# Transposing the widening layers' outputs on VectorE instead of TensorE

## The chip, the cores and the metric

The kernel runs on one core of a Trainium2 chip, in one launch. The metric is the device time of one execution in microseconds (us). The matrix products run on TensorE (PE; its weight loads are listed apart as PEld), the elementwise work on VectorE (DVE) and ScalarE (ACT), a few small things on GpSimd (POOL), and the weights come in over DMA queues that SyncE (SP) starts.

## The reference

Two transformer blocks are computed one after the other on 256 tokens of width 2048, all in float32. What matters for this change are the two feed-forward parts, one at the end of each block; everything else (gated linear attention, forgetting attention, sparse attention, pooling, memory attention) is left as it is.

```
h = h + (o * gate) @ w_out
u = jax.nn.relu(rms_norm(h, mlp_norm_g) @ w_up)          # 2048 -> 8192
h = h + (u * u) @ w_down                                  # 8192 -> 2048
...
h = rms_norm_2(x, ln_ffn_pre[l])
y = (jax.nn.silu(h @ w_gate[l]) * (h @ w_up[l])) @ w_down[l]   # 2048 -> 5632 -> 2048
x = x + rms_norm_2(y, ln_ffn_post[l])
```

## The kernel before

**The products.** Every weight matrix is read once from HBM, in units of 1024 columns per partition (two blocks of 128 rows by 512 columns, 512 KB). A unit lands in one of five raw buffers (`raw`), ScalarE rounds it into `wh` (line 133, type float32r), VectorE computes the rest `wl = raw - wh` (line 366), and the pair goes into one of six pairs of buffers. The activations are split into a high part H and a low part L in the same way. TensorE then does three products for each block and each half of the tokens: H by wh (line 460), H by wl (461) and L by wh (462), each 128x512. A unit is therefore 2 blocks x 2 halves x 3 = 12 matmuls. The pair is free for a later unit when its last matmul (462) is done.

**The feed-forward parts.** The first one (`up`, `down`) has 16 groups `up0` to `up15` of 512 output columns, each with 16 blocks (8 units), and after every second pair of them a set of four groups `dn` with 16 units, in which the outputs of an earlier pair are multiplied by `w_down`. So the outputs of `up` groups 2b and 2b+1 are used after the groups 2b+2 and 2b+3 have been multiplied. The second part (`ffn_gate`, `ffn_up`, `ffn_down`, names `fg`, `fu`, `fd`) has 11 groups of gate and up columns and is arranged in the same way.

**What is transposed.** A widening group leaves its result with the tokens on the partitions, and the narrowing product needs it with the columns on the partitions. So each of the 27 outputs (16 + 11), 256 tokens by 512 columns, goes through `T_split`: in two halves, four transposes each of a 128x128 block on TensorE into a PSUM bank `pb` (line 203), then a copy to the high part by ScalarE (`split_T`, `self.act(hi, ps)`) and a subtraction for the low part by VectorE (`self.tt(lo, ps, hi)`), both 128x512 out of PSUM. Before it, `up` applies Relu on ScalarE (two 128x512) and squares on VectorE (128x1024); `ffn_up` multiplies on VectorE.

**The order.** The program is written out by a Python planner. The matmuls of the products follow a fixed list of units. Between two blocks `pump` advances tasks (Python generators; a `yield` ends a step), guarded by rough costs (`dv`, `act`, `tr`) that the planner adds up for each engine: it takes steps of a task while the planned times of ScalarE and VectorE are less than 3500 ns ahead of the planned time of TensorE. `more` splits the next units, up to four ahead of the one in use. Each engine then runs its own instructions strictly in that order, and waits at semaphores for the others. Scratch tiles `s` of 128x1024 come from an arena of 32.

Of the kernel before, what the change touches and what calls it, by code (L numbers as in the profile page):

```python
# [10 lines left out]
F32 = mybir.dt.float32  # L11
F32R = mybir.dt.float32r
I32 = mybir.dt.int32
AF = mybir.ActivationFunctionType
OP = mybir.AluOpType
# [93 lines left out]
class Program:  # L109
# [399 lines left out]
    def T_split(self, nat, gain, hi, lo):  # L509
        h3, l3 = v3(hi, 4), v3(lo, 4)  # L510

        def sink(half, ps):
            s = slice(2 * half, 2 * half + 2)
            self.split_T(ps, None if gain is None else gain[:, s], h3[:, s], l3[:, s])

        yield from self.T_group(nat, sink)

    def T_plain(self, nat, dst, gain=None):
        d3 = v3(dst, 4)

        def sink(half, ps):
            s = slice(2 * half, 2 * half + 2)
            if gain is None:
                self.copy(d3[:, s], ps)
            else:
                self.scopy(d3[:, s], ps, gain)

        yield from self.T_group(nat, sink)
# [59 lines left out]
def v3(f, a):  # L588
    return f.rearrange("p (a b) -> p a b", a=a)


class Kernel(Program):
# [472 lines left out]
    def up(self, banks, j):  # L1065
        yield from self.until(("rs", "h"))
        rs = self.rs["h"]
        (f,) = yield from self.F.wait()
        f3 = v3(f, 2)
        for t in range(2):  # L1070
            self.act(f3[:, t], banks[t], AF.Relu, scale=rs[:, t:t + 1])
        if j == 15:
            self.free_TT("h")
        yield "B"
        self.tt(f, f, f, OP.mult)
        yield 1
        yield from self.u_T(f3, j, 2)
        self.F.put(f)

    def u_T(self, f3, j, per):  # L1080
        h, l = yield from self.R.wait(2)
        yield from self.T_split(f3, None, h, l)
        H, L = self.TT.setdefault(("u", j // per), ([None] * per, [None] * per))
        H[j % per], L[j % per] = h, l
        self.ev.add(("u", j))

    def down(self, banks, b, c):
# [546 lines left out]
    def ffn_up(self, banks, j):  # L1634
        yield from self.until(("g", j))
        f = self.S.pop(("g", j))
        f3 = v3(f, 2)
        for t in range(2):
            self.stt(f3[:, t], banks[t], self.rs["hf"][:, t:t + 1], f3[:, t], OP.mult, OP.mult)
        if j == 10:  # L1640
            self.free_TT("hf")
        yield "B"
        h, l = yield from self.R.wait(2)
        yield from self.T_split(f3, None, h, l)
        self.F.put(f)
        b, k, n = j // 2, j % 2, 2 if j < 10 else 1
        H, L = self.TT.setdefault(("w", b), ([None] * n, [None] * n))
        H[k], L[k] = h, l
        self.ev.add(("w", j))
# [109 lines left out]
    def build(self):  # L1759
# [105 lines left out]
        def inter(up, dn, nb, per):  # L1865
            seq = list(up(0))
            for b in range(nb):
                seq += list(up(b + 1)) if b + 1 < nb else []
                seq += dn(b)
            return seq  # L1870
# [276 lines left out]
```

## Time and profile before

| | |
|---|---|
| median of 3 runs | 2641.49 us (2641.45 to 2643.71) |
| the profiled execution | 2642.02 us |
| its span in the profile | 2640.3 us |
| PE busy | 2616.5 us (99%), 12196 matmuls |
| DVE busy | 1504.9 us (57%), 1921 instructions |
| ACT busy | 1251.9 us (47%), 1708 instructions |
| POOL busy | 76.5 us (3%) |
| DMA, mean | 189 GB/s |
| granted TensorE clock, mean | 0.998 |

The span runs from the first to the last instruction of the program, and the execution's own time is 1.7 us longer. A share of busy time is a mean over the whole span. A matmul's duration is its way through the pipeline, so consecutive matmuls overlap; how fast TensorE really goes is read from the distance between starts in the timeline. A row of the timeline gives the start, the time, the engine, the line, the operation, out<-in and a count, and in brackets the idle time of the engine before it and what ended that.

### The profile page before, as it was taken

To read this page: it belongs to the slowest core of one execution; us is meant where nothing else is said; L and a number is where in the kernel's file an instruction comes from. 1 tells how busy PE (TensorE), PEld (TensorE's weight loads), DVE (VectorE), ACT (ScalarE), POOL (GpSimd) and SP (SyncE) were. 2 spreads that over 40 slices of the span, in tenths; PEclk is the share of its full clock that TensorE was granted. 3 is DMA by queue.
4 is the path that set the end of the run, shared out by engine and by line. 5 is a ranking of instruction groups with operands and counts; after the bars stand their busy time and mean duration, and the time that the engine had idled before them with its cause. 6 is when DMAs were issued, how large, how long until landed. Compare 5 with 4: busy or idle time off the path is not lost.

```text
span 2640.3 us, 32053 instructions
## 1 busy us (share of the span) xinstructions
PE 2616.5 (99%) x12196; PEld 2168.9 (82%) x12196; DVE 1504.9 (57%) x1921; ACT 1251.9 (47%) x1708; POOL 76.5 (3%) x97
## 2 busy tenths in 40 slices
PE   9999999999999999999999999999999999999998
PEld 7888888888888888888888888888788888888886
DVE  6567655555555555555566545666755455555555
ACT  7544544444444444444455344465554444444443
POOL 0001000000000000001000000000100000000001
PEclk9999999999999999999999999999999999999999
DMA  9643565555566565555444557555455555556553
GB/s 343 204 139 119 166 216 185 188 188 184 191 201 223 187 223 195 191 202 198 150 143 147 190 177 258 201 199 184 136 193 189 192 188 194 186 195 202 195 186 129
DMA packets 138891, 500.18 MB, mean 189 GB/s; under 512 B 15650, under 2 KB 16594, under 8 KB 138737
## 3 DMA queue, kind: packets, MB, share of 16 engines
q1 hardware_dynamic: 131760, 473.16, 53.0%
q0 software_dynamic: 6976, 24.98, 2.7%
q8 instruction: 95, 1.56, 0.2%
q14 instruction: 60, 0.48, 0.1%
HBM read 493.33 MB, written 7.88 MB: 190 GB/s over the span
## 4 chain that ended last, share of the span: by engine, by line
PE 94%; issue 4%; DVE 1%; ACT 0%; DMA 0%; POOL 0%; SPq 0%; DVEq 0%; ACTq 0%; POOLq 0%
PE gb L460 29%; PE gb L462 29%; PE gb L461 29%; PE pb L197 4%; PE pb L203 3%; DVE wl L366 0%; DVE s L169 0%; DMA s<-memT 0%; DVE s L158 0%; POOL st L232 0%; ACT wh L133 0%; PE gb L451 0%; ACT s L133 0%; PE gb L450 0%; PE gb L452 0%
## 5 line engine op out<-in xcount | busy, mean ns | idle before, releaser
L366 DVE TENSOR_TENSOR wl<-raw,wh 128x1024 fp32r<-128x1024 f32 (+1 forms) x876 | 1052.8, 1219 | 689.5 <-ACT wh L133 687.4
L460 PE MATMUL gb<-wh,s 128*128 128x512 f32 x3496 | 1383.9, 396 | 2.2 <-ACT wh L133 2.1
L461 PE MATMUL gb<-wl,s 128*128 128x512 f32 x3496 | 1362.5, 390 | 2.5 <-DVE wl L366 2.5
L462 PE MATMUL gb<-wh,s 128*128 128x512 f32 x3496 | 1363.4, 390 | 0.0
L133 ACT ACTIVATE wh<-raw 128x1024 fp32r<-128x1024 f32 (+1 forms) x878 | 914.0, 1055 | 802.2 <-PE gb L462 766.8
L462 PEld LDWEIGHTS gb<-wh,s 128*128 128x128 f32 x3496 | 656.4, 188 | 139.3 <-DVE s L169 0.5
L460 PEld LDWEIGHTS gb<-wh,s 128*128 128x128 f32 x3496 | 657.2, 188 | 137.4 <-ACT wh L133 3.7
L461 PEld LDWEIGHTS gb<-wl,s 128*128 128x128 f32 x3496 | 657.5, 188 | 135.1 <-DVE wl L366 4.2
L158 DVE TENSOR_TENSOR s<-gb,s 128x512 f32<-128x512 f32 x144 | 98.1, 691 | 159.6 <-PE gb L462 130.5
L133 ACT ACTIVATE s<-pb 128x512 fp32r<-128x512 f32 (+4 forms) x171 | 89.4, 536 | 163.6 <-PE pb L203 139.5
L133 ACT ACTIVATE s<-gb,st 128x512 f32<-128x512 f32 (+1 forms) x112 | 70.0, 642 | 199.5 <-PE gb L462 188.0
L197 PE MATMUL pb<-s,s 128*128 128x128 f32 (+4 forms) x720 | 116.5, 301 | 1.3 <-DVE s L158 0.9
L203 PE MATMUL pb<-cc,s 128*128 128x128 f32 x700 | 106.0, 274 | 5.4 <-DVE s L169 5.3
L203 PEld LDWEIGHTS pb<-cc,s 128*128 128x128 f32 x700 | 87.0, 141 | 29.0 <-DVE s L169 6.6
L197 PEld LDWEIGHTS pb<-s,s 128*128 128x128 f32 x720 | 97.7, 191 | 9.5 <-DVE s L158 1.3
L158 DVE TENSOR_TENSOR s<-pb,s 128x512 fp32r<-128x512 f32 (+4 forms) x87 | 57.5, 664 | 62.4 <-ACT s L133 58.6
L133 ACT ACTIVATE s<-pb,vecs 128x256 fp32r<-128x256 f32 (+2 forms) x109 | 42.3, 453 | 49.9 <-PE pb L203 40.5
L163 DVE TENSOR_SCALAR s<-gb,st 128x512 f32<-128x512 f32 (+1 forms) x32 | 20.9, 658 | 67.8 <-PE gb L462 51.5
L169 DVE SCALAR_TENSOR_TENSOR s<-pb,vecs,s 128x256 fp32r<-128x256 f32 (+1 forms) x104 | 40.0, 435 | 29.0 <-ACT s L133 29.0
L133 ACT ACTIVATE s<-s,st 128x128 f32<-128x128 f32 (+2 forms) x73 | 32.8, 450 | 31.7 <-DVE st L163 30.4
L133 ACT ACTIVATE s<-s 128x512 f32<-128x512 f32 (+3 forms) x46 | 37.0, 807 | 21.5 <-DVE s L158 12.4
L232 POOL TENSOR_TENSOR st<-st,nhalf 128x8 f32<-128x8 f32 (+2 forms) x21 | 26.1, 1243 | 689.5 <-DVE st L165 689.5
(113 smaller groups left out, 565.0 us busy)
## 6 DMA issues: line engine op xcount, KB each, us to landing
raw<-w_in SPq DMA_DIRECT2D x216, 512.0 KB, 4.2
raw<-w_up SPq DMA_DIRECT2D x216, 512.0 KB, 4.4
raw<-w_down SPq DMA_DIRECT2D x216, 512.0 KB, 4.4
raw<-w_gate SPq DMA_DIRECT2D x88, 512.0 KB, 4.6
raw<-w_out SPq DMA_DIRECT2D x32, 512.0 KB, 4.5
raw<-w_mix_out SPq DMA_DIRECT2D x32, 512.0 KB, 4.6
raw<-w_br_pool SPq DMA_DIRECT2D x16, 512.0 KB, 5.2
raw<-w_br_attn SPq DMA_DIRECT2D x16, 512.0 KB, 4.1
```

Of the source, the lines that this page charges most:

```text
L133: self.nc.scalar.activation(out, in_, func, **kw)
L158: self.nc.vector.tensor_tensor(out, a, b, op)
L163: self.nc.vector.tensor_scalar(out, a, s1, None, op0=op0)
L169: self.nc.vector.scalar_tensor_tensor(out, a, s, b, op0, op1)
L197: self.nc.tensor.matmul(out, lhsT, rhs, start=start, stop=stop)
L203: self.nc.tensor.transpose(out, in_, self.ident[:k, :k])
L232: self.nc.gpsimd.tensor_tensor(r, t, self.nhalf[:, :k], op=OP.pow)
L366: self.nc.vector.tensor_sub(l[:, :m], r, h[:, :m].bitcast(F32))
L460: mm(o, H[:, c:c + 128], wh, start=st, stop=False)
L461: mm(o, H[:, c:c + 128], wl, start=False, stop=False)
L462: mm(o, L[:, c:c + 128], wh, start=False, stop=sp)
```

## The change

A new function `T_dve` takes the place of `T_split` for the 27 outputs. It takes one more scratch tile `g`, and fills it with 16 transposes on VectorE. Each reads 32 partitions (quarter `a` of the tokens of a half) and 256 elements of each (8 pieces of 32), turns each block of 32 by 32, and writes it to 32 partitions of quarter `q` of `g`. After every second of them the step ends. Then ScalarE makes the high part from `g` and VectorE the low part, now 128x1024 in one piece and out of SBUF. In `up` the square is taken on ScalarE and no longer on VectorE.

```
+    def T_dve(self, f, hi, lo):
+
+        (g,) = yield from self.F.wait()
+        x = f.rearrange("p (t k q j) -> p k t q j", t=2, k=4, q=4)
+        y = g.rearrange("p (k t a i) -> p k t a i", k=4, t=2, a=4)
+        for a in range(4):
+            for q in range(4):
+                self.nc.vector.transpose(y[32 * q:32 * q + 32, :, :, a], x[32 * a:32 * a + 32, :, :, q])
+                self.dv(256)
+                if q % 2:
+                    yield 1
+        self.F.put(f)
+        self.act(hi, g)
+        yield 1
+        self.tt(lo, g, hi.bitcast(F32), OP.subtract)
+        self.F.put(g)
...
     def up
-        self.tt(f, f, f, OP.mult)
+        self.act(f, f, AF.Square)
         yield 1
-        yield from self.u_T(f3, j, 2)
-        self.F.put(f)
...
+        yield from self.T_dve(f, h, l)
...
     def ffn_up
-        yield from self.T_split(f3, None, h, l)
-        self.F.put(f)
+        yield from self.T_dve(f, h, l)
```

On TensorE the order of the changed kernel is the order before without 54 rows of four transposes; no other row moves there. POOL's and SP's orders are the same. The place shown on TensorE is the first half of the output of `up0`, between two products of 128x512 (`gb` is a product's PSUM bank, `wh` and `wl` the weight pair, `cc` holds the identity, `s_115` is the output of `up0`):

```order
 L462 MATMUL gb_83<-wh_70,s_108_2865 128x512
-L203 MATMUL pb_87<-cc,s_115_3407 128x128 x4
 L460 MATMUL gb_82<-wh_72,s_109_3006 128x512
 L461 MATMUL gb_82<-wl_73,s_109_3006 128x512
```

The row of four transposes is gone and the products close up.

On VectorE the same place, the output `s_115` of `up0`, reads before (the square, then the two low parts `s_117` out of the banks `pb`, among the low parts `wl` of the weights):

```order
L366 TENSOR_TENSOR wl_77<-raw_69,wh_76 128x1024
L158 TENSOR_TENSOR s_115_3407<-s_115_3407 128x1024
L366 TENSOR_TENSOR wl_79<-raw_65,wh_78 128x1024
L366 TENSOR_TENSOR wl_81<-raw_66,wh_80 128x1024
L158 TENSOR_TENSOR s_117_3442<-pb_87,s_116_3441 128x512
L158 TENSOR_TENSOR s_117_3442<-pb_89,s_116_3441 128x512
L366 TENSOR_TENSOR wl_71<-raw_67,wh_70 128x1024
```

and in the changed kernel (`s_118` is the tile `g`, `s_116` the high part):

```order
L366 TENSOR_TENSOR wl_79<-raw_65,wh_78 128x1024
L525 STREAM_TRANSPOSE s_118_3437<-s_115_3407 32x8x32 x2
L366 TENSOR_TENSOR wl_81<-raw_66,wh_80 128x1024
L525 STREAM_TRANSPOSE s_118_3437<-s_115_3407 32x8x32 x4
L366 TENSOR_TENSOR wl_71<-raw_67,wh_70 128x1024
L525 STREAM_TRANSPOSE s_118_3437<-s_115_3407 32x8x32 x4
L366 TENSOR_TENSOR wl_73<-raw_68,wh_72 128x1024
L525 STREAM_TRANSPOSE s_118_3437<-s_115_3407 32x8x32 x2
L366 TENSOR_TENSOR wl_75<-raw_69,wh_74 128x1024
L525 STREAM_TRANSPOSE s_118_3437<-s_115_3407 32x8x32 x4
L366 TENSOR_TENSOR wl_77<-raw_65,wh_76 128x1024
L158 TENSOR_TENSOR s_117_3436<-s_118_3437,s_116_3435 128x1024
```

The square has left this engine, and 16 transposes in pieces of two or four now stand between the low parts of five units of weights, with the low part of the output behind the sixth.

## Rows read from the trace of the kernel before

**Rows 1.** The page's first part: busy time, share of the span and instructions of each engine.

```profile
PE 2616.5 (99%) x12196; PEld 2168.9 (82%) x12196; DVE 1504.9 (57%) x1921; ACT 1251.9 (47%) x1708; POOL 76.5 (3%) x97
```

**Rows 2.** Busy time in two stretches, most of the first feed-forward part and most of the second: the length, then busy us and number of instructions of PE, PEld, DVE, ACT and POOL, the granted clock, the DMA share and GB/s.

```profile
450.00:1110.00 660.00, 660.00 (x2980) 545.94 (x2980) 361.01 (x348) 289.80 (x316) 9.23 (x16) 1.00 0.58 196
1980.00:2580.00 600.00, 600.00 (x2687) 496.97 (x2686) 307.95 (x288) 251.81 (x259) 1.14 (x2) 1.00 0.58 192
```

**Rows 3.** The timeline of PE around the transposes of one output of `up`, from the fourth matmul ahead of the first four transposes to the fifteenth behind the second four.

```profile
1013.65 0.39 PE L461 MATMUL gb<-wl,s 128*128 128x512 f32 x1
...
1014.56 0.39 PE L462 MATMUL gb<-wh,s 128*128 128x512 f32 x1
1014.79 0.60 PE L203 MATMUL pb<-cc,s 128*128 128x128 f32 x4
1015.14 0.48 PE L460 MATMUL gb<-wh,s 128*128 128x512 f32 x1
1015.46 0.40 PE L461 MATMUL gb<-wl,s 128*128 128x512 f32 x1
...
1016.62 0.60 PE L203 MATMUL pb<-cc,s 128*128 128x128 f32 x4
...
1019.12 0.39 PE L460 MATMUL gb<-wh,s 128*128 128x512 f32 x1
```

**Rows 4.** The groups of instructions in the same stretch (1013.83 to 1019.13 us, with the matmul that started at 1013.65 still running): count, busy us and mean ns.

```profile
L460 PE MATMUL gb<-wh,s 128*128 128x512 f32 x7 | 2.9, 415 | 0.0
L462 PE MATMUL gb<-wh,s 128*128 128x512 f32 x7 | 2.8, 393 | 0.0
L461 PE MATMUL gb<-wl,s 128*128 128x512 f32 x7 | 2.7, 391 | 0.0
L203 PE MATMUL pb<-cc,s 128*128 128x128 f32 x8 | 1.2, 272 | 0.0
```

**Rows 5.** The timeline of ACT soon after, with nothing but the weights' high parts to do.

```profile
1021.36 1.06 ACT L133 ACTIVATE wh<-raw 128x1024 fp32r<-128x1024 f32 x1 [1.61 <-PE gb L462]
1024.08 1.06 ACT L133 ACTIVATE wh<-raw 128x1024 fp32r<-128x1024 f32 x1 [1.66 <-PE gb L462]
1026.80 1.06 ACT L133 ACTIVATE wh<-raw 128x1024 fp32r<-128x1024 f32 x1 [1.66 <-PE gb L462]
```

**Rows 6.** The timeline of DVE, from the square of that output to the weights behind it.

```profile
1005.20 1.23 DVE L366 TENSOR_TENSOR wl<-raw,wh 128x1024 fp32r<-128x1024 f32 x1 [1.50 <-ACT wh L133]
1011.21 1.23 DVE L366 TENSOR_TENSOR wl<-raw,wh 128x1024 fp32r<-128x1024 f32 x1 [4.79 <-ACT wh L133]
1012.36 1.22 DVE L158 TENSOR_TENSOR s<-s 128x1024 f32<-128x1024 f32 x1
1013.49 2.35 DVE L366 TENSOR_TENSOR wl<-raw,wh 128x1024 fp32r<-128x1024 f32 x2
```

**Rows 7.** Groups of instructions over the whole span, different shapes apart: count, busy us, mean ns, and idle time of the engine ahead of them with what ended it.

```profile
L366 DVE TENSOR_TENSOR wl<-raw,wh 128x1024 fp32r<-128x1024 f32 x870 | 1048.7, 1222 | 685.7 <-ACT wh L133 683.8 <-issue 0.3
L203 PE MATMUL pb<-cc,s 128*128 128x128 f32 x696 | 105.2, 274 | 5.4 <-DVE s L169 5.3
L158 DVE TENSOR_TENSOR s<-gb,s 128x512 f32<-128x512 f32 x144 | 98.1, 691 | 159.6 <-PE gb L462 130.5 <-ACT junk L133 26.5 <-ACT wh L133 2.4
L133 ACT ACTIVATE s<-pb 128x512 fp32r<-128x512 f32 x78 | 46.7, 599 | 112.8 <-PE pb L203 112.8
L158 DVE TENSOR_TENSOR s<-pb,s 128x512 fp32r<-128x512 f32 x66 | 45.6, 691 | 54.7 <-ACT s L133 54.7
L133 ACT ACTIVATE s<-s 128x1024 f32<-128x1024 f32 x18 | 19.0, 1054 | 15.3 <-DVE s L169 9.0 <-DVE s L158 6.2
L158 DVE TENSOR_TENSOR s<-s,s 64x256 f32<-64x256 f32 x28 | 11.7, 416 | 0.2
L158 DVE TENSOR_TENSOR s<-s,s 128x1024 f32<-128x1024 f32 x9 | 11.0, 1217 | 0.0
L158 DVE TENSOR_TENSOR s<-s,s 128x256 f32<-128x256 f32 x18 | 7.2, 416 | 0.1
L158 DVE TENSOR_TENSOR st<-st,g 128x2 f32<-128x2 f32 x16 | 2.6, 163 | 0.5
```

**Rows 8.** Who waited for the tile `wl` (us, times): PE's weight loads and its matmuls.

```profile
PEld gb L461: 4.2, 5
PE gb L461: 2.5, 4
```

**Rows 9.** The list of waits, three rows: who waited, for whom, us in total, times, the longest.

```profile
ACT wh L133 <- PE gb L462: 766.8, 472, 4.4
DVE wl L366 <- ACT wh L133: 687.4, 489, 6.0
...
ACT wh L133 <- DMA raw<-w_mem_kv: 9.0, 9, 2.4
```

**Rows 10.** Two of the page's DMA issues: KB each and us from issue to landing.

```profile
raw<-w_up SPq DMA_DIRECT2D x216, 512.0 KB, 4.4
raw<-w_down SPq DMA_DIRECT2D x216, 512.0 KB, 4.4
```

More of the change, by code (lines that the diff above doesn't have):

```diff
@@ L1074, in up @@
         yield "B"
-        self.tt(f, f, f, OP.mult)
+        self.act(f, f, AF.Square)
         yield 1
-        yield from self.u_T(f3, j, 2)
-        self.F.put(f)
-    def u_T(self, f3, j, per):
         h, l = yield from self.R.wait(2)
-        yield from self.T_split(f3, None, h, l)
-        H, L = self.TT.setdefault(("u", j // per), ([None] * per, [None] * per))
-        H[j % per], L[j % per] = h, l
+        yield from self.T_dve(f, h, l)
+        H, L = self.TT.setdefault(("u", j // 2), ([None] * 2, [None] * 2))
+        H[j % 2], L[j % 2] = h, l
         self.ev.add(("u", j))
@@ L1643, in ffn_up @@
         h, l = yield from self.R.wait(2)
-        yield from self.T_split(f3, None, h, l)
-        self.F.put(f)
+        yield from self.T_dve(f, h, l)
         b, k, n = j // 2, j % 2, 2 if j < 10 else 1
```

## The prediction

> **What bounds the kernel now.** I read the shares of busy time first, then the two stretches in which the change acts, then the timeline of TensorE in one of them, and last the waits. TensorE is busy 99% of the span [rows 1], and in the two feed-forward stretches 100%, 660.00 of 660 us and 600.00 of 600, at a granted clock of 1.00, while VectorE is busy 361.01 us (55%) and 307.95 us (51%) there [rows 2]. Busy alone doesn't say that TensorE runs at its pace, so look at who waits. ScalarE's high parts of the weights waited 766.8 us for TensorE to free a pair, and for a DMA only 9.0 us; VectorE's low parts waited 687.4 us for ScalarE [rows 9]. In the other direction TensorE waited for the low parts 2.5 us in the whole run and its weight loads 4.2 us [rows 8]. So the chain runs from TensorE outwards: it frees a pair, the others refill it and are idle until the next. What leaves TensorE's queue there leaves the time; what is added to VectorE costs nothing until a low part comes late.
>
> The pace: with nothing but products, ScalarE starts a high part each 2.72 us, always let go by TensorE [rows 5]. A unit is 12 matmuls, so one takes 2.72 / 12 = 0.2267 us, though a row's duration is 0.39.
>
> **What is removed from TensorE.** 27 outputs of 8 transposes, 216 instructions in 54 pieces of four. Their cost is the room they take between starts. Around one piece: the matmul ahead starts at 1014.56, the second one behind at 1015.46 [rows 3]. Without the piece these are two steps, 0.453 us; they took 0.90. So a piece costs 0.447 us, 0.112 a transpose, and 54 pieces 24.1 us. But the pace does not recover at once. From the matmul at 1013.65 to the one at 1019.12 there are 21 products [rows 3, 4], 20 steps, which at 0.2267 would be 4.53 us and took 5.47. So a whole output costs 0.94 us, 0.89 for its two pieces and 0.05 in slightly wider steps behind them, and 27 outputs 25.4 us. I take this one: a step that is wide only behind transposes goes with them. If those wide steps come from something else that stays, it is 24.1.
>
> The orders show that nothing else on TensorE moves. A stall does not go with it: all 696 transposes of this form had 5.4 us of idle time ahead of them [rows 7], and 5.3 us of it was waiting for line 169, a scaling that these outputs don't go through.
>
> **What is added to VectorE.** Per output: 16 transposes of 256 elements per partition on 32 partitions, and one low part 128x1024 in SBUF at 1.22 us; removed are two low parts out of PSUM at 0.69 each, and in `up` the square at 1.22 [rows 6, 7]. No row of before shows a transpose on VectorE. A 256-element operation in SBUF takes 416 ns, on 64 partitions as on 128 [rows 7], so the number of partitions does not matter. From below an instruction of 2 elements takes 163 ns, from above one of four times the elements 1217 ns [rows 7], as if each element took four turns. I take 0.42 us, the row with the same number of elements. Then `up` adds 16 x 0.42 + 1.22 - 1.22 - 1.38 = 5.3 us, `ffn_up` 16 x 0.42 + 1.22 - 1.38 = 6.6 us: 16 x 5.3 + 11 x 6.6 = 157 us more on VectorE, which goes to 446 us in the first stretch (some 69%) and 381 in the second (64%), if all outputs fall in them.
>
> [...]
>
> What hides it: a pair is refilled as soon as it is freed, and it is used again six units later, that is five units or 13.6 us after its release. High part 1.06 us, low part 1.23 us [rows 5, 6], so 2.4 us of the 13.6 are used (the low part starts when the high part is done) and 11 us are spare. The raw buffer is the other way round: freed by the low part, its next load lands 4.4 us later [rows 10] and is wanted 13.6 us after the last, so a lag of VectorE of up to 13.6 - 2.4 - 4.4 = 6.8 us does not even delay a high part.
>
> Locally, the order puts 16 transposes among five units' low parts, and the output's low part behind them: 16 x 0.42 + 6 x 1.22 = 14.0 us in five units of 2.72, 13.6 us. VectorE falls 0.4 us behind, of 11 spare, and catches up in the next unit, where it has 1.5 us idle [rows 6]. So at 0.42 us nothing of it reaches TensorE.
>
> **The rest.** ScalarE loses two copies out of PSUM, 1.20 us, and gains one of 1024 elements, 1.05, and in `up` the square, 1.05 [rows 7]: 16 x 0.9 - 11 x 0.15 = 13 us more, on an engine that is busy 44% in the first stretch [rows 2]. Its new wait, the high part behind the last transpose, holds the next `wh` by as much as VectorE lags, under the same 11 us. The outputs come some 10 us later than before, but are multiplied two groups later in `up` (16 units, 43.5 us) and no sooner in the rest: no cost. The tile `g` is one more of 32. All these I set to nothing.
>
> **The sum.** 2642.0 - 25.4 = 2616.6 us for the profiled execution. It lies 0.5 us above the median of the runs, so for the median 2616.1 us.
>
> **Rivals.**
>
> *VectorE falls too far behind (slower).* If a transpose costs c, two neighbouring outputs of `up` are the tightest place: from the first transpose of the one to the last of the other are 8 + 5 units, 35.4 us, in which VectorE has 32 c + 15 x 1.22 = 32 c + 18.3 us. With 11 us spare TensorE waits from c = 0.88 us on, and loses 32 us for each us of c beyond, in 8 pairs. The outputs of `ffn_up` are twice as far apart: 16 c + 7.3 against 13.6 + 11, so from c = 1.08 on, 16 us per us in 11 outputs. The gain is used up at 256 x (c - 0.88) = 25.4, c = 0.98. At the upper bound, c = 1.22, it is 256 x 0.34 + 176 x 0.14 = 112 us: 2616 + 112 = 2728 us. For it: reading pieces of 32 and writing other partitions is no operation that the trace shows. Against it: this takes more than twice the row with the same element count. Between 0.88 and 0.98 the gain shrinks, from 2616 to 2641.
>
> *Transposes are worth more than their room.* If what counts were the duration in the row, 274 ns [rows 7], 216 of them would be 59 us, and the time 2583 us. Against it: the products around four transposes close up to 0.447 us [rows 3], and durations overlap. [...]
>
> *Something else paces the feed-forward parts.* If the loads did (58% of the DMA engines' time there, 196 GB/s [rows 2]), the room would stay empty and the time be 2642 us. Against it: ScalarE waited 9.0 us in all for a load [rows 9].
>
> *The pace of the products falls,* because VectorE is in SBUF more. One per cent on the 1260 us of both stretches is 12.6 us, half the gain: 2629 us. Against it: from 1013.65 to 1014.56 VectorE works all the time, and four steps take 0.91 us, as where it has idle time [rows 3, 5, 6].
>
> **Chances.** The forecast (VectorE hidden, 24 to 25.4 us gained, give or take 1) 0.83; part of the gain lost to lag or pace, 2619 to 2635 us, 0.07; nothing gained 0.02; VectorE too far behind, slower, 0.06; more than 30 us gained 0.02. The likeliest case's own range is 2614.5 to 2619. A range for 8 times in 10 takes in a bit of the partial case: 2613 to 2626 us. A measurement of this kernel can tell some 0.2%, 5.3 us, from no change. Faster by more than that: 0.83 + 0.06 of the partial case + 0.02 = 0.91. Within it: 0.01 + 0.02 = 0.03. Slower: 0.06.
>
> **What would show it.** TensorE has 216 matmuls less and the same 0.2267 us step through every output; its busy share stays at 99%. VectorE has 432 rows of line 525 at about 0.42 us, and TensorE's waits for `wl` stay under some 10 us. A mean of over 0.88 us at line 525, with new waits of TensorE for `wl` in the `up` part, would prove the forecast wrong by the first rival; a step above 0.23 us through the feed-forward parts, the pace; a gain under 20 us without either, that I have missed a stall.

## The result, and the profile after

The changed kernel takes 2617.7 us (median of 4 runs, 2616.85 to 2619.07); before, in the same rounds, 2642.31 us (4 runs). The ratio is 0.9906 with a 95% interval of 0.9894 to 0.9918: 25 us faster, and 21.7 to 28.0 by the interval. The forecast was 2616.1 us, in a range of 2613 to 2626. The profiled execution took 2616.85 us against 2642.02, 25.2 us less where the sum said 25.4.

The page of the changed kernel, its span and first part, answers to [rows 1]:

```profile
span 2615.1 us, 31982 instructions
PE 2591.0 (99%) x11980; PEld 2148.5 (82%) x11980; DVE 1670.6 (64%) x2310; ACT 1264.2 (48%) x1697; POOL 76.6 (3%) x97
```

TensorE has 216 matmuls less and is 25.5 us less busy, which is the time gained; its share is still 99%. VectorE has 165.7 us more, ScalarE 12.3 us more. So 178 us of work on two engines bought 25 us, because only the third one counts. By stretch, busy time of PE, PEld, DVE, ACT and POOL and the granted clock (the second stretch begins 25 us earlier than in [rows 2]):

```profile
450.00:1100.00 650.00, 650.00 (x2875) 537.87 (x2874) 451.73 (x569) 304.07 (x317) 9.23 (x16) 1.00 0.60 200
1955.00:2555.00 600.00, 600.00 (x2649) 497.04 (x2648) 377.98 (x438) 254.05 (x252) 1.15 (x2) 1.00 0.59 195
```

TensorE is busy without a gap in both; VectorE went from 55% to 69% and from 51% to 63%.

The groups of instructions of the changed kernel, shapes apart, answer to [rows 7]:

```profile
L366 DVE TENSOR_TENSOR wl<-raw,wh 128x1024 fp32r<-128x1024 f32 x870 | 1053.6, 1223 | 568.6 <-ACT wh L133 562.0 <-issue 0.3
L525 DVE STREAM_TRANSPOSE s<-s 32x256 f32<-32x256 f32 x432 | 188.2, 436 | 7.8
L133 ACT ACTIVATE s<-s 128x1024 fp32r<-128x1024 f32 x29 | 30.8, 1061 | 68.5 <-DVE s L525 68.5
```

The operation that no row of before showed takes 436 ns; the estimate was 416 to 420. VectorE still sits idle 562 us waiting for ScalarE's high parts, so the new work went into that idle time. ScalarE's new wait, for the last transpose ahead of the high part, is 68.5 us in 27 outputs, and nobody on the path notices it.

Who waited for the tile `wl`, after, as in [rows 8]:

```profile
PEld gb L461: 3.8, 4
PE gb L461: 2.5, 4
```

TensorE waits no longer than before. The same place as in [rows 3], in the changed kernel: VectorE's timeline through the first output of `up`, and TensorE's first and last rows of the same stretch.

```profile
500.08 0.87 DVE L525 STREAM_TRANSPOSE s<-s 32x256 f32<-32x256 f32 x2
500.98 1.23 DVE L366 TENSOR_TENSOR wl<-raw,wh 128x1024 fp32r<-128x1024 f32 x1
502.24 1.78 DVE L525 STREAM_TRANSPOSE s<-s 32x256 f32<-32x256 f32 x4
504.06 1.23 DVE L366 TENSOR_TENSOR wl<-raw,wh 128x1024 fp32r<-128x1024 f32 x1
...
513.53 1.22 DVE L158 TENSOR_TENSOR s<-s,s 128x1024 fp32r<-128x1024 f32 x1
```

```profile
499.48 0.39 PE L461 MATMUL gb<-wl,s 128*128 128x512 f32 x1
...
512.85 0.39 PE L460 MATMUL gb<-wh,s 128*128 128x512 f32 x1
```

VectorE has no bracket in these rows, so it works without a pause from 500.1 to 514.7 us: it is locally full, as the working said, and a little more (14.7 us of work where 14.0 were worked out, against 13.6). TensorE makes 59 steps in the 13.37 us between its two rows, 0.2266 us each. The wide steps that stood behind the transposes are gone too. The two matmuls that open and close [rows 3] are now here:

```profile
1000.93 0.39 PE L461 MATMUL gb<-wl,s 128*128 128x512 f32 x1
...
1005.46 0.39 PE L460 MATMUL gb<-wh,s 128*128 128x512 f32 x1
```

The 20 steps between them take 4.53 us where they took 5.47. Laying the two traces side by side, matmul by matmul, gives the same at every output: each of the 27 is worth 0.94 us (0.939 to 0.942).

### The profile page after: what moved, and what is told of

It reads as the page before. It is cut to its first block, busy times and chain, and to the rows that moved or that the text cites. A ratio compares the mean times of both kernels' runs of the same rounds, so it can differ in the third digit from the quotient of the medians.

```text
span 2615.1 us, 31982 instructions
## 1 busy us (share of the span) xinstructions
PE 2591.0 (99%) x11980; PEld 2148.5 (82%) x11980; DVE 1670.6 (64%) x2310; ACT 1264.2 (48%) x1697; POOL 76.6 (3%) x97
## 4 chain that ended last, share of the span: by engine, by line
PE 94%; issue 4%; DVE 1%; ACT 0%; DMA 0%; POOL 0%; SPq 0%; DVEq 0%; ACTq 0%; POOLq 0%
PE gb L460 29%; PE gb L462 29%; PE gb L461 29%; PE pb L197 4%; PE pb L203 2%; DVE s L169 0%; DVE wl L366 0%; DMA s<-memT 0%; DVE s L158 0%; ACT wh L133 0%; POOL st L232 0%; PE gb L450 0%; ACT s L133 0%; PE gb L452 0%; PE gb L451 0%
## 5 line engine op out<-in xcount | busy, mean ns | idle before, releaser
L525 DVE STREAM_TRANSPOSE s<-s 32x256 f32<-32x256 f32 x432 | 188.2, 436 | 7.8
L133 ACT ACTIVATE s<-s 128x1024 fp32r<-128x1024 f32 (+3 forms) x89 | 82.5, 928 | 90.0 <-DVE s L525 68.5
L133 ACT ACTIVATE s<-pb 128x512 f32<-128x512 f32 (+4 forms) x117 | 56.9, 506 | 73.9 <-PE pb L203 49.7
L203 PE MATMUL pb<-cc,s 128*128 128x128 f32 (+1 forms) x484 | 73.2, 274 | 5.6 <-DVE s L169 5.6
L203 PEld LDWEIGHTS pb<-cc,s 128*128 128x128 f32 (+1 forms) x484 | 59.7, 141 | 22.4 <-DVE s L169 6.9
L158 DVE TENSOR_TENSOR s<-s,s 128x60 f32<-128x60 f32 (+5 forms) x123 | 73.8, 633 | 0.6
```

What stands on the lines that cost most here:

```text
L133: self.nc.scalar.activation(out, in_, func, **kw)
L158: self.nc.vector.tensor_tensor(out, a, b, op)
L203: self.nc.tensor.transpose(out, in_, self.ident[:k, :k])
L525: self.nc.vector.transpose(y[32 * q:32 * q + 32, :, :, a], x[32 * a:32 * a + 32, :, :, q])
```

## The experiments

**One part alone, and the other.** Two kernels take the new function in one feed-forward part only.

```
 up only, in ffn_up:
-        yield from self.T_dve(f, h, l)
+        yield from self.T_split(f3, None, h, l)
+        self.F.put(f)
```

> Only the 16 outputs of up are transposed on VectorE; the 11 of the second feed-forward part go back to TensorE. Room theory: an output is worth 0.94 us of TensorE's queue, so 16 x 0.94 = 15.0 us less than before, about 2627 us where before is 2642. If instead the up part lost something to a lagging VectorE (its outputs stand closest together), the gain would be under 13 us and TensorE would wait for wl there.

```
 second part only, in up:
-        self.act(f, f, AF.Square)
+        self.tt(f, f, f, OP.mult)
         yield 1
         h, l = yield from self.R.wait(2)
-        yield from self.T_dve(f, h, l)
+        yield from self.T_split(f3, None, h, l)
+        self.F.put(f)
```

> Only the 11 outputs of the second feed-forward part are transposed on VectorE; the 16 of up are as before, square included. Room theory: 11 x 0.94 = 10.3 us less than before, about 2632 us. With the run of the up outputs alone the two gains add up to that of the whole change, 25 us; if part of the gain came from elsewhere (ScalarE's and VectorE's reads of PSUM spread over both), they would not.

Measured: `up` only 2628.78 us (4 runs), second part only 2632.61 us (4 runs), before 2643.67 us (13 runs on that chip). The gains are 14.9 us (ratio 0.9946, 0.9931 to 0.9961) and 11.1 us (0.9961, 0.9946 to 0.9976), where 15.0 and 10.3 were expected. Together they make 26.0 us, that of the whole change within the intervals. The gain goes by the number of outputs, and neither part shows a cost of its own, as far as intervals of 4 us to either side can tell.

**The work moved, but the room not freed.** All of the change is made, and TensorE does its 216 transposes all the same, into banks that nobody reads.

```
 T_dve, at its start:
+        nat = v3(f, 2)
+        def pe(half, b):
+            for k in range(2):
+                for t in range(2):
+                    c = (2 * half + k) * 128
+                    self.tr(b[:, k * 256 + t * 128:k * 256 + t * 128 + 128], nat[:, t, c:c + 128])
+        yield from self.pipe([0, 1], [(pe, [lambda half, b: None])])
```

> The whole change, but the 216 transposes stay on TensorE too, into PSUM banks that nobody reads; VectorE's and ScalarE's work is that of the changed kernel. Room theory: all of the gain is TensorE's queue, so the time is that of before, 2641 to 2643 us. Rival, that part of the gain comes from VectorE and ScalarE no longer reading the transposes out of PSUM, or from a shorter chain: 2620 to 2635 us.

Measured: 2643.28 us (10 runs), ratio to before 1.0001 (0.9992 to 1.0011). The busy times of this kernel:

```profile
PE 2616.7 (99%) x12196; PEld 2168.6 (82%) x12196; DVE 1670.1 (63%) x2310; ACT 1263.2 (48%) x1697; POOL 76.5 (3%) x97
```

VectorE and ScalarE are as busy as in the changed kernel, TensorE as in [rows 1], and the time is that of before. This is the sharpest run: to within its interval, some 3 us, the whole gain is room in TensorE's queue, and the work added elsewhere is worth nothing in either direction.

**The square back on VectorE.**

```
 up
-        self.act(f, f, AF.Square)
+        self.tt(f, f, f, OP.mult)
```

> The whole change, but the square in up stays on VectorE (1.22 us more there for each of 16 outputs, 1.05 us less on ScalarE). Theory of hidden work: the same time as the changed kernel, 2616 to 2619 us. Rival, that VectorE is near its limit in the up part and the move of the square is what kept it under: 16 x 1.2 = up to 19 us more, 2620 to 2636 us.

Measured: 2620.78 us in one run, 3 us more than the changed kernel's median. To see whether the up part lost them, take the first and last start of the transposes: in the changed kernel, in this one, and in a second profiled run of the changed kernel (2619.24 us, of the runs behind the last experiment).

```profile
L525 DVE STREAM_TRANSPOSE s<-s x432: 425/436/445, 500.1 to 2555.8; 32x256 f32<-32x256 f32 x144
```

```profile
L525 DVE STREAM_TRANSPOSE s<-s x432: 425/436/443, 503.0 to 2559.8; 32x256 f32<-32x256 f32 x144
```

```profile
L525 DVE STREAM_TRANSPOSE s<-s x432: 424/436/442, 503.0 to 2558.2; 32x256 f32<-32x256 f32 x144
```

The first transpose comes 2.9 us later, and so it does in the second run of the changed kernel: this is a difference from run to run, not one of the square. From the first transpose to the last it is 2055.7, 2056.8 and 2055.2 us. Against the changed kernel's first run TensorE's matmuls keep the same distance, 2.5 us, through the whole up part. So the up part lost nothing of the 19 us of the rival, and moving the square was not needed for the gain.

**How much more VectorE can take.** Each transpose is issued two or three times in a row, or every second one twice, with the planner's costs left alone.

```
-                self.nc.vector.transpose(y[32 * q:32 * q + 32, :, :, a], x[32 * a:32 * a + 32, :, :, q])
+                for _ in range(2):        # 3; 1 + q % 2
+                    self.nc.vector.transpose(y[32 * q:32 * q + 32, :, :, a], x[32 * a:32 * a + 32, :, :, q])
```

> The whole change with each transpose on VectorE issued twice in a row (32 for an output, the second writing the same values again), the planner's costs unchanged. By the prediction's working TensorE waits from 0.88 us for the pair on: at 2 x 0.436 = 0.87 us it is at the edge, 2617 to 2622 us. If the second of a pair starts before the first has ended (as two low parts of the weights in a row do, 0.09 us early), the pair is 0.79 us and nothing is lost, 2617 us. If there is no such slack (the rival: VectorE's 64% are already the limit), 432 x 0.44 = 190 us more.

> The whole change with each transpose issued three times in a row. By the prediction's working: at 3 x 0.436 = 1.31 us the loss is 256 x (1.31 - 0.88) + 176 x (1.31 - 1.08) = 151 us, about 2768 us; if repeats start 0.09 us early, 1.13 us for the three, 256 x 0.25 + 176 x 0.05 = 73 us, about 2690 us. TensorE's waits for wl grow from 2.5 us by that much. If the slack is larger than the 11 us that I worked out, less than 40 us are lost.

> The whole change with every second transpose issued twice (24 for an output, the planner's costs unchanged). With the spacing that the runs show, 0.45 us a transpose and 1.25 us for a low part between them: the four outputs of up0 to up3 in a row need 96 x 0.45 + 29 x 1.25 + some 6 = 85 us on VectorE where TensorE takes 29 units, 79 us: a lag of 6 us, under the 11 that are spare, so the time is that of the changed kernel, 2616 to 2620 us. Rival, that the spare time is a few us only, as the 43 us lost with doubled transposes could also mean: 20 us more, about 2638 us, with TensorE waiting for wl in the up part.

Measured, one run each: half again 2618.42 us, twice 2660.38 us, three times 2857.58 us. The kernel with half again was made when the other two had been measured, and is as expected. Those two lost far more than they should, 43 and 240 us against 5 and 151 at most. TensorE's waits for the low parts of the weights, from the lists of the kernel with two and of the one with three:

```profile
PE gb L461 <- DVE wl L366: 27.6, 18, 3.1
```

```profile
PE gb L461 <- DVE wl L366: 141.6, 88, 4.1
```

They were 2.5 us before [rows 8], so the mechanism is the rival's, and its place too: with doubled transposes the second feed-forward part stays whole (2000 to 2600 us: TensorE busy 600.00 of 600), and the up part alone loses. What was wrong is the size. VectorE's timeline of that kernel, from the first transpose of one output to the last of its neighbour:

```profile
828.92 1.23 DVE L366 TENSOR_TENSOR wl<-raw,wh 128x1024 fp32r<-128x1024 f32 x1 [0.67 <-ACT wh L133]
830.07 1.81 DVE L526 STREAM_TRANSPOSE s<-s 32x256 f32<-32x256 f32 x4
831.90 1.23 DVE L366 TENSOR_TENSOR wl<-raw,wh 128x1024 fp32r<-128x1024 f32 x1
833.16 3.66 DVE L526 STREAM_TRANSPOSE s<-s 32x256 f32<-32x256 f32 x8
...
854.04 1.22 DVE L366 TENSOR_TENSOR wl<-raw,wh 128x1024 fp32r<-128x1024 f32 x1 [0.64 <-ACT wh L133]
855.93 1.23 DVE L366 TENSOR_TENSOR wl<-raw,wh 128x1024 fp32r<-128x1024 f32 x1 [0.67 <-ACT wh L133]
...
866.98 1.29 DVE L158 TENSOR_TENSOR s<-gb,s 128x512 f32<-128x512 f32 x2
...
870.13 1.22 DVE L366 TENSOR_TENSOR wl<-raw,wh 128x1024 fp32r<-128x1024 f32 x1
...
877.62 1.84 DVE L526 STREAM_TRANSPOSE s<-s 32x256 f32<-32x256 f32 x4
```

It is 49.4 us from 830.07 to 879.46, for 13 units of 2.72 us, 35.4 us on TensorE. The prediction's working puts 46.1 us there, at 0.87 us for a transpose issued twice. Transposes follow each other at 0.46 us (eight in 3.66) and not at 0.436, a pair of additions of a `dn` group that stands among them had been left out, and VectorE itself is held twice by some 0.65 us, because ScalarE waits for its last transpose (9.88 us ahead of 849.90) and then has several high parts to catch up; on the other side, one of the 15 low parts counted falls behind the stretch.

The spare time was put too high as well. TensorE's rows at its first wait there, and at the same wait for the next two pairs of outputs:

```profile
868.68 0.39 PE L460 MATMUL gb<-wh,s 128*128 128x512 f32 x1
871.41 0.50 PE L461 MATMUL gb<-wl,s 128*128 128x512 f32 x1 [2.34 <-DVE wl L366]
...
963.10 0.80 PE L461 MATMUL gb<-wl,s 128*128 128x512 f32 x1 [2.36 <-DVE wl L366]
...
1054.78 0.52 PE L461 MATMUL gb<-wl,s 128*128 128x512 f32 x1 [2.34 <-DVE wl L366]
```

The wait at 871.41 ends with the low part begun at 870.13, the eleventh behind the one at 828.92. Without it TensorE would have been there at 868.91, and 11 units earlier, at 839.0, it would have wanted the low part that VectorE had finished at 830.15. So 8.8 us were spare at this place, not 11. The lag goes on growing behind this wait, and what two neighbouring outputs lose is read from wait to wait: 91.69 and 91.68 us for 32 units, which are 87.0 us at 2.72. That is 4.6 us, where the prediction's formula gives 32 x 0.04 = 1.3 us for 0.92 in place of 0.88. Against the changed kernel, matmul by matmul, six pairs of outputs lose 27 us in this way. The other 16 us are lost in `up0` to `up3`: the sets `dn` stand behind the second pair and behind every pair from there on, so these are four outputs in a row and not two, and the lag adds up over them.

**Another quarter, or the same one.** Each transpose writes to the quarter of the partitions that it reads; number and size stay.

```
-                self.nc.vector.transpose(y[32 * q:32 * q + 32, :, :, a], x[32 * a:32 * a + 32, :, :, q])
+                self.nc.vector.transpose(y[32 * a:32 * a + 32, :, :, q], x[32 * a:32 * a + 32, :, :, q])
```

> Each of the 16 transposes writes to the same quarter of the partitions that it reads, so the blocks land in the wrong places and the output is not the reference's; number and size of the instructions are the same. Time: that of the changed kernel, 2616 to 2619 us, since VectorE is hidden. Row by row: if going to another quarter makes an instruction wait for the end of the one before, groups of four now take 0.436 + 3 x 0.35 = 1.5 us in place of 1.78; if not, 1.78 as before.

Measured: 2617.26 us, and in VectorE's timeline

```profile
500.95 0.75 DVE L525 STREAM_TRANSPOSE s<-s 32x256 f32<-32x256 f32 x2
...
502.74 1.52 DVE L525 STREAM_TRANSPOSE s<-s 32x256 f32<-32x256 f32 x4
...
510.43 1.43 DVE L525 STREAM_TRANSPOSE s<-s 32x256 f32<-32x256 f32 x4
```

In the changed kernel four transposes go to another quarter three times and take 1.78 us. Here the four at 502.74 do it once, in their middle, and take 1.52; the four at 510.43 stay in one quarter and take 1.43. So going to another quarter costs some 0.1 us each time. From start to start it is (1.78 - 0.436) / 3 = 0.45 us in the changed kernel, no less than one transpose takes, as if the instruction waited for the one before; here the median row takes 398 ns, and within a quarter it is (1.43 - 0.40) / 3 = 0.34 us from start to start. The repeats of the doubled kernel stay in a quarter too and show no such gain (eight took 3.66 us, 0.46 us from start to start); no run shows why. On the kernel's time the quarter has no effect.

**Going on with it.** Does the same pay for other outputs? One kernel adds 9 of them (`gq`, `gk`, `mk`, `mq`, `fq`, `fk` and three chunks of the residual behind `w_out`), one adds 6 more that stand closer to their use.

```
 headnorm_T, plain_T (of gq and gk)
-        yield from self.T_plain(v3(f, 2), o, gain)
+        yield from self.T_quarters(f, o)      # the 16 transposes of T_dve
+        self.act(o, o, scale=gain)            # headnorm_T only
 norm_T, for "h" and c < 3 (further 6: for "h2" and c < 2, and so in gate, grp < 2, and br, c < 2)
-        yield from self.T_split(f3, self.vec(gain, 4 * c, 4), h, l)
+        yield from self.T_dve_gain(f, self.vec(gain, 4 * c, 4), h, l)   # T_dve with a gain; merged branches: T_dve
```

> The changed kernel itself, timed beside the next two on the same chip: 2616 to 2619 us.

> The changed kernel, and 9 more outputs are transposed on VectorE in the same way: the keys and queries of the first block (gq, gk, mk, mq, fq, fk) and the first three chunks of the residual behind w_out. 18 more pieces of four leave TensorE: 9 x 0.94 = 8.5 us less than the changed kernel, about 2609 us, if they too are hidden. Rival, that VectorE is too full in the first block (64% on the mean, with attention's work among it) or that the longer way to the transposed tile makes attention and up0 wait: 2615 to 2630 us.

> As the run with 9 more outputs, and 6 further ones: two of the linear attention's, two chunks of the residual behind the last w_down of the first block, and two of the merged branches of the second. 30 pieces of four leave TensorE: 15 x 0.94 = 14.1 us less than the changed kernel, about 2603 us. These come at shorter distances from their use (10.9 us of units each), so the rival is that a part is given back as waits of TensorE for the transposed tiles: 2605 to 2620 us.

Measured on one chip, 4 runs each: the changed kernel 2619.27 us, 9 more 2609.79 us, 15 more 2626.44 us; before 2643.33 us. Nine more outputs gain 9.5 us, where 8.5 were expected: the version with 9 more is faster than both kernels (ratio to before 0.9875, 0.9860 to 0.9889). Six further ones lose 16.7 us in place of gaining 5.6, 22.3 us short. TensorE's timeline of that kernel shows where, at the end of the first block and behind the merged branches:

```profile
1167.63 1.50 PE L203 MATMUL pb<-cc,s 128*128 128x128 f32 x4 [2.96 <-DVE s L158]
...
1173.02 0.79 PE L462 MATMUL gb<-wh,s 128*128 128x512 f32 x1 [2.19 <-DVE s L169]
```

```profile
1681.57 0.50 PE L462 MATMUL gb<-wh,s 128*128 128x512 f32 x1 [2.02 <-DVE s L158]
...
1695.56 0.79 PE L460 MATMUL gb<-wh,s 128*128 128x512 f32 x1 [6.18 <-ACT s L133]
1698.81 0.79 PE L462 MATMUL gb<-wh,s 128*128 128x512 f32 x1 [2.04 <-DVE s L158]
```

TensorE waits for scratch tiles `s` of VectorE and ScalarE, and not for `wl`. The first row is a transpose left on TensorE, whose input, a sum of VectorE, stands behind VectorE's transposes of other outputs; in the other four rows a product waits for a transposed operand. The kernel with 9 more has none of these waits. With one of 0.47 us at 1169.60 they make 15.9 us, all in these two places, so it is the chunks of the residual and the merged branches that pay for the longer way, and the two outputs of the linear attention show no wait. The other 6 us fit the clock in the two places (the third figure from the end of these rows is the granted clock, 0.80 in both), where for part of the time TensorE's steps are wider: seven of 0.427 us from 1682.64 to 1685.63, in place of 0.2267:

```profile
1160.00:1185.00 25.00, 19.25 (x73) 14.52 (x72) 20.86 (x40) 12.55 (x23) 5.35 (x8) 0.80 0.76 260
1675.00:1710.00 35.00, 24.76 (x97) 19.13 (x97) 24.65 (x37) 15.40 (x22) 2.11 (x4) 0.80 0.53 180
```

Which of the four outputs does it wasn't tried apart.

## Why the prediction was right

- *The bound.* That TensorE's pace sets the feed-forward parts rested on who waits for whom, and the run with both kinds of transposes confirms it: the same work on VectorE with TensorE's queue unchanged gives the time of before, 1.0001.
- *The room of a transpose.* 0.94 us per output was read from the starts around one output, and each of the 27 gave 0.94. So the extra 0.05 us of wide steps went too, as assumed, and the rival that took the row's duration, 59 us, is out. That the profiled runs show 25.2 us of 25.4 is nearer than the working could promise: ahead of the first output the changed kernel was 0.5 us early, between the two parts it lost 0.7 us, both where the kernels are the same. Nine other outputs gave 9.5 us of 8.5, with times that scatter by 2 us.
- *VectorE hidden.* 436 ns against 420; 166 us more against 157, 7 of the 9 from these 16 ns; 69% and 63% of the two stretches against 69 and 64. TensorE's waits for `wl` stayed at 2.5 us.
- *The rest.* ScalarE 12 us more against 13, all hidden; the longer way of the outputs cost nothing in these 27, since two groups stand between them and their use. The run with 15 more shows that this was an argument of its own, not a matter of course.
- *The rival on the other side.* Its mechanism and place were right, its size was not: the point from which TensorE waits was put at 0.88 us a transpose. With two issues of 0.46 us, 0.92, 43 us are lost where its own formula gives 10, and at 1.5 issues nothing. The steps that failed are the 46 us of VectorE's work for two neighbours (49.4 measured), the 11 us of spare time (8.8 where it was measured), and that `up0` to `up3` were taken for pairs. The forecast did not depend on it, since at 0.44 us a transpose TensorE's waits stayed where they were.

## What to carry to other kernels

Where one engine's queue is full, price an instruction on it by the room between starts. On an engine that was idle because it waited for the full one, instructions cost nothing here as long as they fitted into that idle time (ratio 1.0001 with the work added and the room not freed): 16 instructions of 0.44 us there were cheaper than 8 of 0.11 us here. Before moving more, work out the spare time of the buffers between the two engines and add up every instruction of the receiving engine in the fullest stretch, then look at how soon the result is wanted: with 9 more outputs the move went on paying, and with 15 more it took back more than those had gained.

## What was not expected of the hardware

A wait was followed by slower steps. With doubled transposes the longest wait of TensorE, 3.12 us, is followed by steps of 0.427 us in place of 0.2267:

```profile
595.47 0.80 PE L461 MATMUL gb<-wl,s 128*128 128x512 f32 x1 [3.12 <-DVE wl L366]
596.07 0.63 PE L462 MATMUL gb<-wh,s 128*128 128x512 f32 x1
596.50 0.63 PE L460 MATMUL gb<-wh,s 128*128 128x512 f32 x1
...
600.76 0.58 PE L461 MATMUL gb<-wl,s 128*128 128x512 f32 x1
601.18 0.40 PE L462 MATMUL gb<-wh,s 128*128 128x512 f32 x1
```

In that stretch the granted clock is 0.52 on the mean, and 0.2267 / 0.427 is 0.53; from 580 to 592, ahead of the wait, with TensorE busy 11.93 of 12 us, it is 1.00:

```profile
580.00:592.00 12.00, 11.93 (x53) 9.36 (x51) 11.50 (x21) 6.09 (x6) 0.00 (x0) 1.00 0.60 189
594.00:601.00 7.00, 5.53 (x13) 4.37 (x14) 6.68 (x12) 0.00 (x0) 0.00 (x0) 0.52 0.40 126
...
866.00:886.00 20.00, 16.92 (x70) 12.35 (x69) 19.36 (x31) 5.88 (x6) 0.00 (x0) 1.00 0.44 143
...
958.00:978.00 20.00, 17.48 (x70) 13.67 (x69) 19.37 (x30) 5.92 (x6) 0.00 (x0) 0.91 0.45 146
```

The length of the wait did not decide it here. Of the waits of 2.34 to 2.36 us in the up part, the one at 871.41 has the full pace behind it (1.00 in the row from 866), and the one at 963.10 some eight slow steps (0.91 on the mean in the row from 958).

Nor are the slow steps paid on top here. From the wait at 871.41, with the full pace behind it, to the one at 963.10 it is 91.69 us, and from there to the one at 1054.78, with the slow steps, 91.68. VectorE sets the pace in both, and catches up while TensorE is slow: of the four small waits behind 871.41, the longest 0.41 us at 884.25, only one of 0.16 us is left behind 963.10.

Over the run the mean granted clock fell from 0.998 to 0.994 with two issues and to 0.975 with three. How much of the 240 us of the latter is the clock's wasn't taken apart.

The second surprise is that the changed kernel's transposes in a row do not overlap on VectorE, while two low parts in a row do: two of 1.22 us took 2.35 [rows 6], but four transposes of 0.436 took 1.78, more than four times one. Writing all four to the same quarter brought them to 1.43.
